# Moving the norms after the attention heads and the SSD into the load of the output projection, and adding the latents' expert rows in halves of 512 columns

## The chip, the core and the metric

The kernel runs on one core of a Trainium2 chip. The metric is the device time of one execution in microseconds; the median of three runs of the kernel before is 2430.44 us. TensorE (PE) does matrix products and transposes, VectorE (DVE), ScalarE (ACT) and GpSimd (POOL) do elementwise work, and SyncE (SP) issues most transfers. Each engine works through its own queue in order. 16 DMA engines move the data; transfers that add to memory or gather rows by an index are issued from POOL and have a queue of their own, the software queue.

## What is computed

Two layers over 512 latent tokens and 256 context tokens of width 1024. Each layer has a mixer and a mixture of experts. Cut to what matters here:

```python
o    = diff_attend(q, k_all, v_all, lam)                 # 4 heads, 128 wide: softmax 1 - lam * softmax 2
attn = rmsnorm(o, subln_w) * (1.0 - lam_init)            # a norm over each head's 128 columns
g    = (y * silu(z)).reshape(..., 2, 256)                # SSD output, gated, two groups
ssd  = g * rsqrt(mean(g * g) + EPS) * ssd_norm_w         # a norm over each group's 256 columns
x    = x + g1 * (concat([attn, ssd]) @ w_out)            # one output projection
x    = x + g2 * sum over experts of gate * down(silu(gate_proj(xe)) * up_proj(xe))
```

Each of 16 experts takes the 64 latent tokens and, in layer 0, the 32 context tokens that score highest, and its rows are added back at these tokens' places. Layer 1 needs no context output.

## The kernel before

**Order of the work.** Tokens lie in tiles of 128: tiles 0 to 3 are latents, 4 and 5 context. A mixer runs in stages: norm and transposes of the input, the columns of the SSD part, the gate `z`, then for each of four heads the projection (`Head.proj`), rotation (`Head.rope`) and attention (`Head.attend`), and at last the output projection (`op_tile`) with residual, norm and router. The order is made by hand: side work is written as generators, and `Slots.tick` advances every live generator by one step per tick while it puts the main products of the stage between them. A generator that yields `STEP` goes on within the same tick, so several chains of small operations are issued in turns. `attend` of head h runs during the projection of head h + 1, that of head 3 during the output projection.

**The root chain.** `rsqrt_steps` (L191 to L217) computes an inverse square root on VectorE in ten small dependent operations, with a `STEP` after each.

**The norms.** At the end of `attend`, ScalarE scales the head's 128 columns by the softmax's denominator (L1832) and sums their squares (L1834); a root chain `ors` on one column follows, and one VectorE operation multiplies by root and weight (L1837). The result is stored to `mixd` in DRAM; head 3's latent tiles are transposed and split at once instead. `z_out` (L1124) does the same for two groups of 256 SSD columns of one tile, with the chain `yrs` and two multiplies (L1135), which run beside the next chunk's `G` (L1072, L1074), the operand of `yd` on TensorE (L1081).

**The output projection.** `op_in` (L1180) loads a tile's mix from `mixd`, transposes it (`mtr`, L1192) and splits it in two float32r parts, hi and lo (L1194, L1196), since each product is three float32r products. It is queued for the next tile while this one is multiplied; the first tile's goes out as the stage starts. `w_out` comes through `Pieces`: ScalarE copies a piece of 128 x 512 to hi (L129), and POOL or VectorE, in turns, subtracts to get lo (L137). Products go over k in the order `OUT_ORDER`, SSD rows of `w_out` (k = 4 to 7) first, head rows (0 to 3) after.

**The experts.** `moe` streams all weights of each expert through SP's queue, in buffers that come free as TensorE uses them. The down projection `yl` (L1536) puts its 64 latent rows as two groups of 32 tokens by four column quarters of 256: each quarter has 32 partitions, the two groups lie side by side in 512 columns. `add_rows` (L1662) then scales one group's 128 x 256 by the gate and `G2` (L1665) and adds it with one indirect transfer of 128 rows of 1 KB (L1666). So an expert makes two such adds for the latents, one for the context in layer 0. Two adds to the same tensor wait for each other.

Of the kernel before, what the change touches and what calls it, by code (L numbers as in the profile page):

```python
# [8 lines left out]
F32 = mybir.dt.float32  # L9
F32R = mybir.dt.float32r  # L10
# [27 lines left out]
R_N1, R_N2, R_CW, R_CB, R_L = 0, 8, 16, 40, 48  # L38
# [26 lines left out]
OUT_ORDER = (4, 5, 6, 7, 0, 1, 2, 3)  # L65
# [47 lines left out]
class Pieces:  # L113
# [7 lines left out]
    def fetch(self):  # L121
        f = next(self.todo, None)
        if f:
            self.raw.append(f(self.net.rawp.tile([P, 512], F32, tag="raw", name="raw", bufs=4)))

    def pull(self, hi, lo):
        self.turn += 1
        nc, x = self.net.nc, self.raw.pop(0)
        nc.scalar.copy(hi.bitcast(F32R), x)  # L129
        self.flush()  # L130
        self.low = (nc.gpsimd if self.turn % 2 or x.shape[-1] == 384 else nc.vector), lo, x, hi

    def flush(self):

        if self.low:
            e, lo, x, hi = self.low
            e.tensor_tensor(lo.bitcast(F32R), x, hi, op=OP.subtract)  # L137
            self.low = None
            self.fetch()


class Net:
# [122 lines left out]
    def consts(self, p1):  # L265
# [8 lines left out]
        for l in range(2):  # L274
# [5 lines left out]
            self.lds(stack[b + R_CB:b + R_CB + 8], rows(I["conv_b"][l]))  # L280
        self.lds(self.rev, I["k_rev"])
# [89 lines left out]
    def pieces(self, l):  # L371
# [22 lines left out]

        cbs = [cb for g in range(2) for _, cb in GROUP[g]]
# [7 lines left out]
        for b in range(2):  # L403
            yield from (cols(w_out, k, 512 * b) for k in OUT_ORDER)

# [285 lines left out]
    def layer_params(self, l, lp, p1, lam_init):  # L691
# [7 lines left out]
        self.wsub = lp.tile([P, P], F32, name="wsub")  # L699
        self.wssd = lp.tile([P, 512], F32, name="wssd")  # L700
# [9 lines left out]
        ld(self.wsub, bc(I["subln_w"][l:l + 1], P))  # L710
        ld(self.wssd, bc(I["ssd_norm_w"][l:l + 1], 512))
# [6 lines left out]

        nc.vector.tensor_scalar(self.wsub, self.wsub, 1.0 - lam_init, None, op0=OP.mult)
# [404 lines left out]
    def z_out(self, l, t, ap):  # L1124

        nc, y = self.nc, self.Y[:, t]
        ss = ap.tile([P, 2], F32, tag="yss", name="yss", bufs=2)
# [8 lines left out]
        self.st(self.mixd[l][t * P:(t + 1) * P, 512:1024], y)  # L1136
# [43 lines left out]
    def op_in(self, l, t, op, psp):  # L1180
# [6 lines left out]
        self.mT[t] = mT = [op.tile([P, KD, P], F32, tag=f"mT{j}", name="mT", bufs=2) for j in range(2)]  # L1187
        yield
        for a, n in ((4, 4), (0, n)):
# [4 lines left out]
            nc.scalar.copy(mT[0][:, c].bitcast(F32R), tr)  # L1194
            yield STEP
            nc.vector.tensor_tensor(mT[1][:, c].bitcast(F32R), tr, mT[0][:, c], op=OP.subtract)  # L1196
# [124 lines left out]
    def route_open(self, l):  # L1321

        cst = self.cst
        self.gidx = cst.tile([96, NE], I32, name=f"gidx{l}") if l == 0 else None
        self.gidc = cst.tile([32, NE], I32, name=f"gidc{l}") if l == 0 else None
        self.sidx = cst.tile([P, 3, NE], I32, name=f"sidx{l}")
        self.gate = cst.tile([P, 3, NE], F32, name=f"gate{l}")
# [28 lines left out]
    def route_b(self, l, psp):  # L1356
# [25 lines left out]
        ps = psp.tile([P, 2, 2, NE], F32, tag="tr", name="sgp", bufs=3)  # L1382
        for g in range(2):
            for j in range(4):
                nc.tensor.matmul(ps[32 * j:32 * j + 32, g].rearrange("p i e -> p (i e)"), self.ident[0:64, 32 * g:32 * g + 32],
                                 c.rearrange("p i e -> p (i e)"), start=True, stop=True, skip_group_check=True)
        nc.vector.tensor_scalar(self.gate[:, 0:2], ps[:, :, 0], 0.5, None, op0=OP.mult)
        for j in range(4):
# [499 lines left out]
```

## Time and profile before

| | |
|---|---|
| median of 3 runs (lowest, highest) | 2430.44 us (2430.13, 2430.88) |
| the profiled execution's time | 2429.65 us |
| its span, first to last instruction | 2427.9 us |
| TensorE matmul busy | 2175.3 us, 90% |
| VectorE busy | 995.3 us, 41% |
| ScalarE busy | 635.9 us, 26% |
| POOL busy | 480.9 us, 20% |
| granted TensorE clock, mean | 0.964 |
| moved by DMA | 702.46 MB, 289 GB/s over the span |

Busy shares are means over stages that have different limits. A transfer's issue and its landing are two moments; what waits for a transfer waits for the landing. A wait that is put down to an engine is put down to what came last by the profile.

### The profile page before, as it was taken

What the parts mean: (1) busy time and instruction counts of PE and PEld (TensorE: products, weight loads), DVE (VectorE), ACT (ScalarE), POOL (GpSimd) and SP (SyncE); (2) the same over time, 40 slices, a digit from 0 to 9 for tenths busy, and PEclk for the clock granted to TensorE, in tenths of its full rate; (3) what the DMA queues carried; (4) which work ended last, traced back from release to release, by engine and by line L of the source; (5) the groups of instructions that cost most, each with busy time, mean ns of one, the idle gap of its engine ahead of it and who ended that gap; (6) DMA issues with size and microseconds to landing.
All of it is one profiled execution on the core that took longest, in us unless ns stands there. A gap on an engine that the chain in (4) does not pass through costs nothing. (4 is left out here: it accounts for less than half of the span.)

```text
span 2427.9 us, 55950 instructions
## 1 busy us (share of the span) xinstructions
PE 2175.3 (90%) x23460; PEld 1335.8 (55%) x23460; DVE 995.3 (41%) x3088; ACT 635.9 (26%) x1739; POOL 480.9 (20%) x584
## 2 busy tenths in 40 slices
PE   6898988998999999999987988989799999988775
PEld 4677787785445455455444667887543333333332
DVE  5789589873111111111116787887611111111010
ACT  4334467521111111111113443565111010101000
POOL 4464233100111101101103464241000001000001
PEclk9999999999999999999998998999899999999998
DMA  7322723678999999999994325324999999999997
GB/s 255 85 76 83 267 63 99 207 249 330 393 403 405 390 401 393 398 395 399 394 388 122 92 58 192 111 71 150 361 370 414 408 411 408 414 409 409 409 412 275
DMA packets 234759, 702.46 MB, mean 289 GB/s; under 512 B 30860, under 2 KB 88412, under 8 KB 234508
## 3 DMA queue, kind: packets, MB, share of 16 engines
q1 hardware_dynamic: 220428, 681.43, 72.6%
q0 software_dynamic: 14080, 17.46, 3.9%
q8 instruction: 185, 3.03, 0.5%
q14 instruction: 66, 0.54, 0.1%
HBM read 675.05 MB, written 23.76 MB: 288 GB/s over the span
## 5 line engine op out<-in xcount | busy, mean ns | idle before, releaser
L1490 PE MATMUL gl<-gw,xeT 128*32 128x512 f32 (+1 forms) x8192 | 655.6, 466 | 62.9 <-DMA gw<-w_up 62.7
L1490 PEld LDWEIGHTS gl<-gw,xeT 128*32 128x32 f32 x8192 | 277.7, 111 | 441.9 <-issue 404.3
L1529 DVE SCALAR_TENSOR_TENSOR th<-th,gl 128x256 f32<-128x256 f32 (+1 forms) x96 | 37.5, 391 | 702.9 <-ACT th L1528 702.9
L1536 PE MATMUL yl<-rt,hl 128*32 128x256 f32 x4080 | 247.5, 380 | 13.6 <-PE gl L1490 9.2
L1528 ACT ACTIVATE th<-gl 128x256 f32<-128x256 f32 (+1 forms) x96 | 35.1, 367 | 774.3 <-PE gl L1490 767.7
L171 PE MATMUL pacc<-rt,H 128*128 128x384 f32 (+1 forms) x768 | 206.3, 351 | 4.5 <-ACT V L1719 2.2
L1536 PEld LDWEIGHTS yl<-rt,hl 128*32 128x32 f32 x4080 | 134.1, 110 | 117.8 <-issue 16.0
L1666 POOL DMA_INDIRECT out<-ys,sidx x32 | 49.5, 1546 | 710.7 <-DVE ys L1665 599.1
L1665 DVE SCALAR_TENSOR_TENSOR ys<-yl,gate,G2l 128x256 f32<-128x256 f32 x64 | 28.0, 479 | 361.3 <-PE yl L1536 361.3
L1573 PE MATMUL gc<-gw,xeT 128*32 128x352 f32 x2048 | 170.6, 459 | 0.0
L171 PEld LDWEIGHTS pacc<-rt,H 128*128 128x128 f32 x768 | 137.8, 197 | 18.0 <-issue 6.3
L171 PE MATMUL xacc<-H,rt 128*128 128x512 f32 (+1 forms) x448 | 134.5, 376 | 6.8 <-ACT H L799 6.2
L171 PE MATMUL pacc<-rt,L 128*128 128x384 f32 (+1 forms) x384 | 130.0, 338 | 0.0
L1428 POOL DMA_INDIRECT xe<-xn2d,gidx x16 | 15.1, 944 | 529.4 <-PE xet L1438 389.8
L1443 ACT ACTIVATE xeT<-xet,MC,A 128x64 f32<-128x64 f32 (+1 forms) x256 | 74.3, 424 | 169.2 <-PE xet L1438 169.2
L137 POOL TENSOR_TENSOR rt<-raw,rt 128x384 fp32r<-128x384 f32 (+1 forms) x88 | 100.0, 1162 | 90.9 <-ACT rt L129 90.7
L171 PE MATMUL oacc<-woh,mT 128*128 128x512 f32 x304 | 107.2, 410 | 0.0
L1536 PE MATMUL yl<-wd,hl 128*32 128x256 f32 x1552 | 101.4, 382 | 4.4 <-DMA wd<-w_down 3.8
L1573 PEld LDWEIGHTS gc<-gw,xeT 128*32 128x32 f32 x2048 | 68.6, 110 | 56.2 <-issue 43.9
L171 PEld LDWEIGHTS xacc<-H,rt 128*128 128x128 f32 x448 | 82.2, 197 | 22.3 <-ACT H L799 7.0
L1666 POOL DMA_INDIRECT xr<-ys,sidx x32 | 49.9, 1560 | 194.9 <-DVE ys L1665 109.1
L1805 ACT ACTIVATE e<-sc,nm,rq 128x768 f32<-128x768 f32 (+1 forms) x80 | 72.1, 904 | 49.5 <-DVE nm L1801 46.9
(408 smaller groups left out, 3446.7 us busy)
## 6 DMA issues: line engine op xcount, KB each, us to landing
gw<-w_gate SPq DMA_DIRECT2D x256, 704.0 KB
gw<-w_up SPq DMA_DIRECT2D x256, 704.0 KB
rt<-w_down SPq DMA_DIRECT2D x255, 512.0 KB
wd<-w_down SPq DMA_DIRECT2D x97, 512.0 KB
mr<-w_mod SPq DMA_DIRECT2D x80, 512.0 KB
raw<-w_in SPq DMA_DIRECT2D x48, 256.0 KB
raw<-w_in SPq DMA_DIRECT2D x64, 192.0 KB
RB<-acsd SPq DMA_DIRECT2D x20, 512.0 KB
```

The costliest lines, as they stand in the source:

```text
L137: e.tensor_tensor(lo.bitcast(F32R), x, hi, op=OP.subtract)
L171: self.nc.tensor.matmul(o, a[x].bitcast(F32R), b[y].bitcast(F32R), start=start and i == 0, stop=stop and i == 2, **kw)
L1428: self.nc.gpsimd.indirect_dma_start(out=xe[0:n], out_offset=None, in_=self.xn2d[0:rows], in_offset=bass.IndirectOffsetOnAxis(ap=idx[0:n, e ...
L1443: nc.scalar.activation(xT[:, kk, c:d], tr[:, k, c - a:d - a], AF.Identity, scale=self.A2[:, s, kk:kk + 1], bias=self.MC[:, l, s, 24 + kk:2 ...
L1490: self.nc.tensor.matmul(gl[c][32 * j:32 * j + 32, o:o + n].rearrange("p (u t i) -> p u t i", u=2, i=32), self.xT[:, k, 32 * g:32 * g + 32] ...
L1528: nc.scalar.activation(th, g, AF.Tanh, scale=0.5)
L1529: nc.vector.scalar_tensor_tensor(th, th, 1.0, g, op0=OP.add, op1=OP.mult)
L1536: nc.tensor.matmul(y[32 * j:32 * j + 32], h[:, b], wd[b][:, 256 * j:256 * j + 256], start=new and b == 0, stop=b == NF - 1, skip_group_che ...
L1573: nc.tensor.matmul(gc[u][32 * j:32 * j + 32].rearrange("p (t i) -> p t i", i=32), xT[:, k, 64:96], w, start=k == 0, stop=k == KD - 1, skip ...
L1665: nc.vector.scalar_tensor_tensor(ys, y, self.gate[:, i, e:e + 1], G2, op0=OP.mult, op1=OP.mult)
L1666: nc.gpsimd.indirect_dma_start(out=dst, out_offset=bass.IndirectOffsetOnAxis(ap=self.sidx[:, i, e:e + 1], axis=0), in_=ys, in_offset=None, ...
L1805: nc.scalar.activation(ei[:, 0:w], sc[:, i * w:i * w + w], AF.Exp, scale=rq[:, t, i:i + 1], bias=nm[:, i:i + 1], accum_out=sm[:, i:i + 1])
```

## The change

`attend` and `z_out` no longer norm. They put the mean of the squares in a tile `mss` (128 x 6 tiles x 6 columns: two SSD groups, four heads) and store the bare values. `op_in` computes one root chain over all columns of its tile and scales the loaded mix, column group by column group, on ScalarE before it transposes. The weights go elsewhere: `ssd_norm_w` scales the SSD rows of `w_out` as they are staged, `subln_w` times 1 - lam_init scales the heads' columns after the transpose, where it lies along the partitions. Head 3's latent tiles keep a root chain of their own. `OUT_ORDER` takes SSD and head rows in turn. In the experts, the two halves of the down projection have 64 partitions each (32 per group) and 512 columns, and the latents' rows are added with one transfer of 128 rows of 2 KB. Two small VectorE operations of the attention are merged into their neighbours.

```diff
-OUT_ORDER = (4, 5, 6, 7, 0, 1, 2, 3)
+OUT_ORDER = (4, 0, 5, 1, 6, 2, 7, 3)
     def pull(self, hi, lo):
-        nc.scalar.copy(hi.bitcast(F32R), x)
+        if scale is None or scale is False:
+            nc.scalar.copy(hi.bitcast(F32R), x)
+        else:
+            nc.scalar.activation(hi.bitcast(F32R), x, AF.Copy, scale=scale)
...
+                e.scalar_tensor_tensor(lo.bitcast(F32R), x, scale, hi, op0=OP.mult, op1=OP.subtract)
...
     def consts(self, p1):
+            self.lds(stack[R_MIX + 5 * l:R_MIX + 5 * l + 1], rows(I["subln_w"][l]))
+            self.lds(stack[R_MIX + 5 * l + 1:R_MIX + 5 * l + 5], rows(I["ssd_norm_w"][l]))
...
     def layer_params(self, l, lp, p1, lam_init):
-        ld(self.wsub, bc(I["subln_w"][l:l + 1], P))
-        ld(self.wssd, bc(I["ssd_norm_w"][l:l + 1], 512))
...
     def z_out(self, l, t, ap):
-            nc.scalar.activation(junk, y[:, 256 * g:256 * g + 256], AF.Square, accum_out=ss[:, g:g + 1])
-        yield
-        rs = yield from self.rsqrt_steps(ap, ss, 2, 1.0 / 256, "yrs")
-        for g in range(2):
-            c = slice(256 * g, 256 * g + 256)
-            nc.vector.scalar_tensor_tensor(y[:, c], y[:, c], rs[:, g:g + 1], self.wssd[:, c], op0=OP.mult, op1=OP.mult)
+            nc.scalar.activation(junk, y[:, 256 * g:256 * g + 256], AF.Square, scale=1.0 / 16, accum_out=self.mss[:, t, g:g + 1])
         self.st(self.mixd[l][t * P:(t + 1) * P, 512:1024], y)
+        yield
...
     def op_in(self, l, t, op, psp):
-        yield
+        rs = yield from self.rsqrt_steps(op, self.mss[:, t, 0:n + 2], n + 2, 1.0, f"mrs{n}")
+        yield
+        cuts = [(512, 768), (768, D)] + [(P * h, P * h + P) for h in range(n)]
+        for i, (a, b) in enumerate(cuts):
+            nc.scalar.mul(mx[:, a:b], mx[:, a:b], rs[:, i:i + 1])
+            if i % 2:
+                yield STEP
...
+            else:
+                yield from self.head_split(mT[0][:, c], mT[1][:, c], tr)
+    def head_split(self, hi, lo, x):
+        w = self.wmix[:, 0:1]
+        self.nc.scalar.activation(hi.bitcast(F32R), x, AF.Copy, scale=w)
+        yield STEP
+        self.nc.vector.scalar_tensor_tensor(lo.bitcast(F32R), x, w, hi, op0=OP.mult, op1=OP.subtract)
...
     def route_b(self, l, psp):
-        ps = psp.tile([P, 2, 2, NE], F32, tag="tr", name="sgp", bufs=3)
-        for g in range(2):
-            for j in range(4):
+        ps = psp.tile([P, 2, NE], F32, tag="tr", name="sgp", bufs=3)
+        for j in range(2):
...
     def moe(self, l):
-        dst = [b.rearrange("n (j c) -> (n j) c", c=256) for b in base]
+        dst = [b.rearrange("n (j c) -> (n j) c", c=512 >> i) for i, b in enumerate(base)]
+        def down_lat(y, h, wd, b):
+            for j in range(2):
+                for g in range(2):
+                    nc.tensor.matmul(y[64 * j + 32 * g:64 * j + 32 * g + 32], h[:, g, b], wd[b][:, 512 * j:512 * j + 512],
+                                     start=b == 0, stop=b == NF - 1, skip_group_check=True)
...
-                    for g in range(2):
-                        down(y[:, 256 * g:256 * g + 256], hl[:, g], wd, b, g == 0)
+                    down_lat(y, hl, wd, b)
...
-                for g in range(2):
-                    self.add_rows(mw, y[:, 256 * g:256 * g + 256], g, e, G2[0], dst[0])
+                self.add_rows(mw, y, 0, e, G2, dst)
...
     def rope(self, a):
-        nc.vector.tensor_scalar(self.nrq[:, a:a + 2], rs[:, :, 0:2], -0.125, None, op0=OP.mult)
     def attend(self, t):
-        nc.vector.tensor_tensor(nm, nm, nrq[:, t], op=OP.mult)
+        nc.vector.scalar_tensor_tensor(nm, nm, -1.0, rq[:, t], op0=OP.mult, op1=OP.mult)
-        nc.vector.tensor_tensor(r2, sm[:, 0:1], rr[:, 1:2], op=OP.mult)
-        nc.vector.tensor_tensor(r2, r2, n.nlam, op=OP.mult)
+        nc.vector.scalar_tensor_tensor(r2, sm[:, 0:1], n.nlam, rr[:, 1:2], op0=OP.mult, op1=OP.mult)
...
-        nc.scalar.activation(junk, ob, AF.Square, accum_out=oss)
-        yield
-        ors = yield from n.rsqrt_steps(ap, oss, 1, 1.0 / P, "ors")
-        nc.vector.scalar_tensor_tensor(ob, ob, ors, n.wsub, op0=OP.mult, op1=OP.mult)
-        if self.h == 3 and not ctx:
+        nc.scalar.activation(junk, ob, AF.Square, scale=P ** -0.5, accum_out=oss)
+        yield
+        if own:
+            ors = yield from n.rsqrt_steps(ap, oss, 1, 1.0, "ors")
+            nc.vector.tensor_scalar(ob, ob, ors, None, op0=OP.mult)
```

## Rows read from the trace of the kernel before

**Rows 1.** The page: the span in 40 slices, tenths of DMA busy time.

```profile
DMA  7322723678999999999994325324999999999997
```

**Rows 2.** Busy time by stage; columns in the first row.

```profile
core 0: us, PE busy (x) PEld busy (x) DVE busy (x) ACT busy (x) POOL busy (x), PEclk, DMA share, GB/s
300.00:420.00 120.00, 105.57 (x709) 97.76 (x707) 105.78 (x390) 79.78 (x227) 43.50 (x66) 0.96 0.23 72
...
620.00:1240.00 620.00, 607.30 (x9069) 312.50 (x9065) 89.25 (x221) 84.50 (x273) 74.64 (x53) 0.99 1.03 398
...
1485.00:1640.00 155.00, 138.67 (x1005) 123.53 (x1003) 119.18 (x408) 86.21 (x239) 58.62 (x93) 0.95 0.41 134
...
1800.00:2400.00 600.00, 528.26 (x6571) 224.45 (x6563) 74.24 (x228) 58.19 (x171) 44.77 (x29) 0.99 1.03 410
```

**Rows 3.** TensorE's waits in four mixer stretches: us in total, times, longest.

```profile
PE yd L1081 <- DVE yrs_y L215: 2.6, 2, 2.1
...
PE wtr L1824 <- DVE QL L1778: 6.4, 3, 3.2
...
PE wtr L1824 <- DVE QL L1778: 5.8, 2, 3.4
...
PE mtr L1192 <- DMA mixin<-mixd: 3.2, 1, 3.2
```

**Rows 4.** Timeline, end: start, duration, engine, line, operation, [idle before <- releaser].

```profile
2412.99 0.87 DVE L1665 SCALAR_TENSOR_TENSOR ys<-yl,gate,G2l 128x256 f32<-128x256 f32 x2 [11.14 <-PE yl L1536]
2413.75 1.54 POOL L1666 DMA_INDIRECT out<-ys,sidx  x1 [33.37 <-DVE ys L1665]
2418.38 1.54 POOL L1666 DMA_INDIRECT out<-ys,sidx  x1 [3.09 <-DMA out<-ys,sidx]
```

**Rows 5.** Timeline, border between the layers.

```profile
1279.53 1.57 POOL L1666 DMA_INDIRECT xr<-ys,sidx  x1 [27.19 <-DVE ys L1665]
1284.15 1.56 POOL L1666 DMA_INDIRECT xr<-ys,sidx  x1 [3.05 <-issue]
1288.17 1.75 SPq L154 DMA_DIRECT2D xin<-xr  x4
1292.86 1.22 DVE L836 SCALAR_TENSOR_TENSOR junk<-xin 128x1024 bf16<-128x1024 f32 x1 [2.96 <-DMA xin<-xr]
```

**Rows 6.** DMA: 2034:2038 weights alone; 2043.59:2051.99 one add; 697.59:703.09 one gather.

```profile
DMA packets 341, 1.70 MB, mean 424 GB/s; under 512 B 40, under 2 KB 40, under 8 KB 341
...
q0 software_dynamic: 144, 0.13, 9.7%
...
q0 software_dynamic: 78, 0.32, 16.7%
```

**Rows 7.** Instructions by tile, xcount: ns min/median/max, first and last start.

```profile
L205 DVE TENSOR_TENSOR ors_e<-ors_e,ors_m x40: 150/159/1206, 286.7 to 1695.8; 128x1 f32<-128x1 f32 x40
...
L1837 DVE SCALAR_TENSOR_TENSOR ob<-ob,ors_y,wsub x40: 339/352/1435, 287.9 to 1698.1; 128x128 f32<-128x128 f32 x40
...
L1832 ACT ACTIVATE ob<-po,rr x40: 355/368/381, 283.3 to 1694.2; 128x128 f32<-128x128 f32 x40
```

**Rows 8.** Timeline, SSD gate of layer 1.

```profile
1452.02 0.97 DVE L196 TENSOR_SCALAR yrs_m<-yss 128x2 f32<-128x2 f32 x1
...
1461.16 0.15 DVE L215 SCALAR_TENSOR_TENSOR yrs_y<-yrs_e,yrs_y 128x2 f32<-128x2 f32 x1
...
1461.38 1.94 PE L1081 MATMUL yd<-XS,G 128*128 128x64 f32 x8 [7.29 <-DVE yrs_y L215]
```

**Rows 9.** Timeline, output projection of layer 1, last tile's mix.

```profile
1698.73 0.80 SPq L154 DMA_DIRECT2D mixin<-mixd  x2
...
1710.87 0.63 PE L1192 MATMUL mtr<-ident,mixin 128*128 128x128 f32 x4
```

**Rows 10.** Chain that ended last, start of that projection: start, us, what.

```profile
1636.46 4.54 DMA mixin<-mixd
...
1641.13 1.73 PE mtr L1192 x7
```

More of the change, by code (lines that the diff above doesn't have):

```diff
@@ L403, in pieces @@
         for b in range(2):
-            yield from (cols(w_out, k, 512 * b) for k in OUT_ORDER)
+            yield from (scaled(cols(w_out, k, 512 * b), k - 4) if k > 3 else plain(cols(w_out, k, 512 * b)) for k in OUT_ORDER)
     def staged(self, W, ws, n, hi=None):
@@ L1325, in route_open @@
         self.gidc = cst.tile([32, NE], I32, name=f"gidc{l}") if l == 0 else None
-        self.sidx = cst.tile([P, 3, NE], I32, name=f"sidx{l}")
-        self.gate = cst.tile([P, 3, NE], F32, name=f"gate{l}")
+        self.sidx = cst.tile([P, 2, NE], I32, name=f"sidx{l}")
+        self.gate = cst.tile([P, 2, NE], F32, name=f"gate{l}")
     def affinities(self, l, t, n):
@@ L1507, in moe_open @@
         self.wp = self.tc.alloc_tile_pool(name=f"wd{l}", bufs=1, reuse_waits="tile", side="right")
-        self.G2 = [mw.tile([P, 256], F32, name="G2" + "lc"[s]) for s in range(2 if ctx else 1)]
+        self.G2 = [mw.tile([P, 512 >> s], F32, name="G2" + "lc"[s]) for s in range(2 if ctx else 1)]
         for s in range(2 if ctx else 1):
@@ L1530, in act, with down @@
             nc.vector.tensor_tensor(h, th, u, op=OP.mult)
-        def down(y, h, wd, b, new=True):
+        def down(y, h, wd, b):
             for j in range(4):
                 nc.tensor.matmul(y[32 * j:32 * j + 32], h[:, b], wd[b][:, 256 * j:256 * j + 256],
-                                 start=new and b == 0, stop=b == NF - 1, skip_group_check=True)
+                                 start=b == 0, stop=b == NF - 1, skip_group_check=True)
+        def down_lat(y, h, wd, b):
+            for j in range(2):
+                for g in range(2):
+                    nc.tensor.matmul(y[64 * j + 32 * g:64 * j + 32 * g + 32], h[:, g, b], wd[b][:, 512 * j:512 * j + 512],
+                                     start=b == 0, stop=b == NF - 1, skip_group_check=True)
         xe = None
@@ L1656, in add_last @@
         nc, (ys, g2) = self.nc, self.ytail
-        nc.scalar.activation(ys, y, AF.Copy, scale=self.gate[:, 2, e:e + 1])
+        nc.scalar.activation(ys, y, AF.Copy, scale=self.gate[:, 1, e:e + 1])
         nc.gpsimd.tensor_tensor(ys, ys, g2, op=OP.mult)
-        nc.gpsimd.indirect_dma_start(out=dst[1], out_offset=bass.IndirectOffsetOnAxis(ap=self.sidx[:, 2, e:e + 1], axis=0),
+        nc.gpsimd.indirect_dma_start(out=dst[1], out_offset=bass.IndirectOffsetOnAxis(ap=self.sidx[:, 1, e:e + 1], axis=0),
                                      in_=ys, in_offset=None, compute_op=OP.add)
@@ L1663, in add_rows @@
         nc = self.nc
[L1664 to L1666 removed]
+        ys = mw.tile([P, 512 >> i], F32, tag=f"ys{i}", name="ys", bufs=2)
+        nc.vector.scalar_tensor_tensor(ys, y, self.gate[:, i, e:e + 1], G2[i], op0=OP.mult, op1=OP.mult)
+        nc.gpsimd.indirect_dma_start(out=dst[i], out_offset=bass.IndirectOffsetOnAxis(ap=self.sidx[:, i, e:e + 1], axis=0),
                                      in_=ys, in_offset=None, compute_op=OP.add)
@@ L1693, in open @@
         self.rq = ap.tile([P, NT, 2], F32, tag="rq", name="rq", bufs=2)
-        self.nrq = ap.tile([P, NT, 2], F32, tag="nrq", name="nrq", bufs=2)
         nq = T if self.full else S
@@ L1841, in attend @@
             nc.tensor.transpose(tr, ob, n.ident)
-            n.split(*([m[:, t] for m in n.oT] if n.oT else [m[:, 3] for m in n.mT[t]]), tr)
+            yield from n.head_split(*([m[:, t] for m in n.oT] if n.oT else [m[:, 3] for m in n.mT[t]]), tr)
             return
```

69 lines of the change are left out of this document (39 added, 30 removed).

## The prediction

> **What bounds the kernel now.** I read the 40 slices first. Their DMA line stands at 9 through two long stretches, the two expert stages, and falls to 2 to 7 through most of the two mixers [rows 1]: two kinds of stage with two different limits. The table by stage, read next, says which resource binds where [rows 2]. In the expert stages the DMA share is 1.03, so no engine of the 16 ever rests, at 398 GB/s in layer 0 and 410 GB/s in layer 1. Such a stage ends when its bytes are through: a later start or a byte more moves its end, an idle engine does not. In layer 0 TensorE is nearly full too, 607.3 of 620 us, so a lighter stream can give at most the 12.7 us that it idles there. In the head stages TensorE works 105.6 of 120 us and 138.7 of 155 us with VectorE at 105.8 and 119.2: TensorE leads, and what it loses it loses mostly to VectorE's queue. The waits by pair name it: the transposes `wtr` wait 6.4 and 5.8 us for `QL`, a VectorE result [rows 3]. Each expert stage starts when the mixer before it lets it, so time saved in a mixer goes through to the end.
>
> **The sum, part by part.** It is made against the profiled execution: 2429.65 us, span 2427.9, 0.79 below the median of 2430.44.
>
> *1. The last add of the program.* The last expert's two halves are scaled in 0.87 us together; the first add is issued at 2413.75, and the second only when the first has landed, at 2418.38 [rows 4]. One add of 512 columns waits for both halves of the scaling (2412.99 + 0.87, and the 0.27 that lay between scaling and issue), so it goes out at 2414.13. That is 2418.38 - 2414.13 = 4.2 us earlier. The same row count is written with twice the bytes each; the landing may be some tenths longer. -4.2 (bounds -4.6 and -3.4).
>
> *2. The border between the layers.* The same pair stands at 1279.53 and 1284.15, and the loads of `xin` on SP's queue follow at 1288.17, after the second add has landed; VectorE's first square waits 2.96 us for such a load until 1292.86 [rows 5]. With one add, issued 0.4 us later than the first was, the loads go out about 1284.1 + 0.4, 3.7 us earlier. VectorE still has the last context expert's activation ahead of it, which ends just before that wait began, so no more than those 2.96 us come through. -3.0 (bounds -3.7 and 0).
>
> *3. The streams.* An add takes queue time from the weights. In the 8.4 us around one add the software queue holds 9.7% of 16 engines, 13.0 us for 128 rows of 1 KB: 102 ns a row. A gather of 4 KB rows holds 16.7% of 5.5 us, 14.7 us for 78 packets: 188 ns. Weights alone run at 424 GB/s, 26.5 a DMA engine, 39 ns per KB [rows 6]. Two adds per expert cost 2 x 128 x 102 ns / 16 = 1.63 us of the stream. What a row of 2 KB costs as an add isn't in the trace. If all of the 102 ns belong to the row, one add costs half and 0.82 us per expert are saved; if all belong to the bytes, nothing. Between them: one more KB at 39 ns makes 141 ns and saves 0.50; read and written back, two times 39 more, it makes 180 ns and saves 0.19. I take 0.35, between these two. 30 experts lie in the streams (the last of each layer is in parts 1 and 2): -10.5 (bounds -24.5 and 0). The down projection issues half as many matmuls of twice the width into the same four column groups; I cost it at nothing, since the stream covers it. If it ran 10% off either way it would show only in layer 0's 12.7 us.
>
> The Trainium skill, "DMA: Bandwidth & Descriptors", section Specifications, speaks against this part: it puts the smallest transfer for line rate at 512 B, so rows of 1 KB would already run as fast as the engine can and wider ones gain nothing. The trace does not agree at 1 KB, for this accumulating write at least: 102 ns against the 39 that 1 KB takes among the weights. By the rule the term is 0, by the row it is -10.5.
>
> *4. SSD gate.* `z_out` loses, in 10 tiles (6 + 4), ten root steps of about 0.16 us [rows 7] and two multiplies over 256 columns. They stand in VectorE's queue between the pieces of the next chunk's `G`, which `yd` on TensorE waits for: 7.29 us at 1461.38, put down to the root chain, whose first step starts at 1452.02 and whose last ends at 1461.31 [rows 8]. VectorE never rests between; from each step's start to that of the next instruction the ten take 3.9 us. In layer 0 waits of `yd` are put down to the chain with 2.6 us [rows 3]. The two squares stay, on ScalarE; the store of `Y` comes earlier. -6 (bounds -9 and 0).
>
> *5. Heads.* 32 of 40 `attend` calls lose a chain of ten steps of 159 ns and a multiply of 352 ns [rows 7]: at most 1.94 us each, less where two chains interleave. 18 of them lie in layer 0's head stage and 12 in layer 1's, 35 and 23 us at most, against 105.8 and 119.2 us that VectorE works there [rows 2]. One further small operation goes in each of the 40 calls (`r2`) and 24 times in `rope` (`nrq`). Off the path all this is worth nothing; on it, it can give at most TensorE's idle time, 14.4 and 16.3 us. I take somewhat over half of the waits for `QL` [rows 3], whose work stands behind such chains: -4 and -3, together -7 (bounds -16 and 0).
>
> *6. The load of the output projection.* Added: 10 chains of n + 2 columns (10 x 10 steps of some 0.16 us against 42 x 10 removed) and 52 ScalarE scalings, five or six per tile. A 128-wide ScalarE scaling by a column takes 368 ns [rows 7]; two of 256 lie between that and twice that, so a latent tile pays 1.8 to 2.6 us; I take 2.1. For later tiles this is covered: the mix is requested at 1698.73 and transposed at 1710.87 [rows 9], 12.1 us for a load that takes 4.5 [rows 10]. The first tile has no cover: its transposes start at 1641.13, as the load lands [rows 10], and TensorE has idled 3.2 us for it [rows 3]. Two things change there. The store of head 2's rows, for which this load waits, no longer follows a root chain and its multiply; that is ten steps of 159 ns and 352 ns [rows 7] with gaps, so store and load come some 2 to 3 us earlier. But the new chain stands among the steps of `rope` on VectorE, and behind the scalings on ScalarE wait the copies of `w_out` pieces and the last head's exponentials, which TensorE needs. Gain 2 to 3, price 2.1 plus a chain of 2 to 5 that partly runs while the load does: between -1 and +4 per layer. I take +1.5, so +3.
>
> *7. At nothing.* Staging `w_out`: half of its pieces get a scale on ScalarE, and VectorE's subtraction becomes a multiply and subtract at the same width; neither engine leads in the output projection. The order of k alternates the halves, but both are transposed before the first product either way. Four small loads more on POOL's queue at the start, while it waits for weights; two broadcasts fewer on POOL, two fewer on SP at the border. Three scalings of routing indices and twelve small matmuls fewer, after the choice of experts. A tenth of a microsecond each, either sign.
>
> Sum: -4.2 - 3.0 - 10.5 - 6 - 7 + 3 = -27.7, so 2402 us by the profiled execution's time and 2402.7, rounded 2403, by the median.
>
> **Rivals.**
> A. *The stream gains nothing* (an add's cost goes with its bytes). For it: an add row of 1 KB costs more than twice what 1 KB of weights does, as if it moved its bytes more than once. Against it: the gather's 188 ns for 4 KB. Time: 2403 + 10.5 = 2413. The Trainium skill's rule in part 3 leads to the same time.
> B. *An add costs by its rows*: layer 0 gets at most the 12.7 us, layer 1 15 x 0.82 = 12.3, so -24.5 in place of -10.5: 2389.
> C. *VectorE's work was not what TensorE waited for*: the small steps filled gaps, and the queues are ordered so that other results come no earlier. For it: the waits for `QL` are less than half of what TensorE idles in the head stages [rows 2, 3]. Parts 4 and 5 fall away: 2403 + 13 = 2416.
> D. *Slower: the scalings stand on the path of every tile.* Mechanism: mix, chain, scalings, transposes and split in a row on three queues for each of the 10 tiles, ahead of that tile's products. Price: 2.1 + ten steps with their gaps, 1.9, is 4.0 per tile, 40 us in place of the 3 of part 6: 2403 + 37 = 2440. It decides from 3.1 us per tile on, where it eats all the rest. Against it: the 12.1 us between request and transpose; for it: ScalarE runs its queue in order, and a scaling that waits for its load holds the copies behind it.
>
> **How the numbers follow.** Forecast 0.50, A 0.15, B 0.12, C 0.12, D 0.11. The measurement can tell about 0.2%, 4.9 us, from no change. A, B and C are all faster by more than that; A and C together would give 2426, at the edge, and I put 0.06 on such mixtures as no change, taken from A and C. Slower is D, 0.11 with 0.01 off for its mild form: faster 0.84, same 0.06, slower 0.10. The range reaches from below B, with the heads at their bound, to A and C together: 2384 to 2426; D lies outside.
>
> **What would show it.** Each step has its place in the profile after: one add per expert for the latents, and at the end one between scaling and the last landing; the `xin` loads about 4 us after the last add of layer 0; the software queue's share around one add (part 3: about 23 us of engine time for 128 rows if a row takes 180 ns, 18 if 141, 13 if rival B holds); no wait of `yd` for a root chain; shorter waits of `wtr` for `QL`; the first `mtr` no later against the last projection of head 3 than 3 us more, and no wait of later `mtr` for a scaling. The prediction is wrong if the expert stage takes as long as before (A), if the mixers do (C), or if TensorE waits before each tile's transposes (D).

## The result, and the profile after

The changed kernel takes 2391.27 us (median of 4 runs, 2388.69 to 2393.27) against 2430.28 us of the kernel before on the same chip (2428.93 to 2430.88). The ratio is 0.984, 95% interval 0.9824 to 0.9855: 35 to 43 us faster, 39 in the middle. 2403 were forecast, 27.7 us faster. The profiled execution has a span of 2388.0 us and a time of 2389.74.

**Where the 40 us of the span went.** I took the same landmarks in both traces (first and last start of an operation) and cut the span into stretches between them. The differences add up to 40.0 us, the 39.9 between the spans but for rounding:

| stretch | before, us | after, us | difference | forecast |
|---|---|---|---|---|
| start to first `xacc` | 29.6 | 31.4 | +1.8 | 0 |
| `xacc`, both layers | 226.1 | 227.1 | +1.0 | 0 |
| last `xacc` to last `pacc` (gate, SSD, heads), layer 0 | 258.9 | 242.3 | -16.6 | -13 in |
| the same, layer 1 | 220.4 | 204.5 | -15.9 | both |
| last `pacc` to first `oacc`, both layers | 25.5 | 30.0 | +4.5 | +3 |
| first `oacc` to first add, both layers | 339.7 | 339.2 | -0.5 | 0 |
| first add to last expert's first add (streams) | 1281.9 | 1274.9 | -7.0 | -10.5 |
| border: that add of layer 0 to first `xacc` of layer 1 | 31.7 | 29.1 | -2.6 | -3.0 |
| that add of layer 1 to the end | 14.1 | 9.4 | -4.7 | -4.2 |

The end, the border and the load of the output projection came out nearly as forecast. The streams gave less. The gate, SSD and head stretches gave two and a half times what was forecast.

Each row is one execution. The kernel of experiment 10 below is the changed kernel up to the first add of layer 1, and its trace has 452.1 us in the two gate, SSD and head rows where the kernel after has 446.8, and 344.6 us from first `oacc` to first add in place of 339.2. So some 5 us in such a row are what two executions can differ by, and the +1.8 and +1.0 tell nothing. The streams, the border and the end repeat better: 1274.1 to 1277.9, 27.9 to 29.2 and 9.2 to 9.4 us in the traces of the experiments that leave them alone.

The page after, first the engines, then granted clock and DMA in 40 slices:

```profile
PE 2176.3 (91%) x20620; PEld 1247.0 (52%) x20620; DVE 931.7 (39%) x2586; ACT 652.2 (27%) x1791; POOL 433.5 (18%) x554
...
PEclk9999999999999999999998999999899999999999
DMA  7323723589999999999994226334999999999997
```

The shape is that of [rows 1]: two expert stages with every slice at 9, two mixers between. VectorE works 63.6 us less over the span.

The ends of the stretches in the timeline after (start, duration, engine, line, operation, idle before and its releaser): border, start and end of layer 1's experts, end of the program.

```profile
1260.76 1.55 POOL L1700 DMA_INDIRECT xr<-ys,sidx  x1 [36.56 <-DVE ys L1699]
...
1265.76 2.58 SPq L162 DMA_DIRECT2D xin<-xr  x4
...
1765.52 1.61 POOL L1700 DMA_INDIRECT out<-ys,sidx  x1 [140.74 <-DMA rt<-w_down]
...
2377.56 0.75 DVE L1699 SCALAR_TENSOR_TENSOR ys<-yl,gate,G2l 128x512 f32<-128x512 f32 x1 [10.22 <-PE yl L1572]
2378.59 1.54 POOL L1700 DMA_INDIRECT out<-ys,sidx  x1 [40.97 <-DVE ys L1699]
```

Against [rows 4] there is one add behind one scaling, and the span ends 9.4 us after it, as it ended 9.5 us after the second one before. Against [rows 5] the loads of `xin` follow 5.0 us after the first add, not 8.6.

One add in the stream, the 8.4 us from 1975.60 (software queue: packets, MB, share of 16 engines), and the expert stages by windows:

```profile
q0 software_dynamic: 144, 0.26, 16.9%
```

```profile
606.00:1220.00 614.00, 603.32 (x7856) 268.39 (x7852) 87.86 (x209) 86.08 (x279) 52.90 (x39) 1.00 1.03 401
...
1766.00:2360.00 594.00, 535.02 (x5300) 188.34 (x5296) 71.10 (x210) 56.94 (x168) 22.76 (x15) 0.99 1.02 410
```

16.9% of 16 engines in 8.4 us are 22.7 us of engine time, 177 ns for each of 128 rows of 2 KB, where a row of 1 KB took 102 [rows 6]. An expert's latent adds so cost 1.42 us of the stream in place of 1.63.

TensorE's waits after in the mixers (us in total, times, longest): SSD gate of layer 0, its heads and output projection, then the same two of layer 1:

```profile
PE yd L1098 <- DVE G L1091: 4.7, 4, 3.5
...
PE sc L1828 <- DVE rope L1784: 4.7, 1, 4.7
...
PE mtr L1210 <- ACT mixin L1204: 2.2, 1, 2.2
PE wtr L1855 <- DVE QL L1810: 0.2, 1, 0.2
...
PE yd L1098 <- DVE G L1091: 5.9, 2, 5.2
...
PE mtr L1210 <- ACT mixin L1204: 8.0, 1, 8.0
...
PE wtr L1855 <- DVE QL L1810: 0.2, 1, 0.2
```

The waits of `wtr` for `QL`, 6.4 and 5.8 us before, are 0.2 us each. No `yd` waits for a root chain; what is left are its waits for `G`. In layer 0 it had such waits before, too:

```profile
PE yd L1081 <- DVE G L1074: 7.1, 3, 6.3
```

With this row the waits of `yd` for `G` and the chains were 7.1 and 2.6 us in layer 0 and 7.3 in layer 1 [rows 8], 17.0 in all, and are 10.6 after. The first `mtr` of a layer waits for a scaling, 2.2 and 8.0 us, and in layer 0 the scores of the output projection wait 4.7 us for a step of the rotation (`rope`).

**The head stretches, split.** Busy time from the last `xacc` to the last `pacc`, layer 0 and layer 1 (columns as in [rows 2]: us; PE, PEld, DVE, ACT, POOL busy; PEclk; DMA share; GB/s), the kernel before:

```profile
154.20:413.10 258.90, 236.12 (x1480) 196.93 (x1479) 208.40 (x737) 137.28 (x393) 97.26 (x143) 0.95 0.35 116
1412.60:1633.00 220.40, 194.53 (x1272) 168.76 (x1271) 175.48 (x567) 110.20 (x307) 93.65 (x135) 0.95 0.34 108
```

and the kernel after:

```profile
154.90:397.20 242.30, 228.29 (x1480) 195.17 (x1479) 172.28 (x455) 135.96 (x393) 97.19 (x143) 0.98 0.38 124
1393.40:1597.90 204.50, 188.59 (x1272) 163.63 (x1271) 152.77 (x385) 109.16 (x306) 92.41 (x134) 0.97 0.37 117
```

The first count shows that TensorE does the same 1480 and 1272 matmuls. Its idle time (length less busy) falls from 48.7 to 29.9 us, 18.8 less; but its busy time falls too, from 430.6 to 416.9, 13.8 less, at a granted clock of 0.98 and 0.97 in place of 0.95. VectorE's busy time falls from 383.9 to 325.1.

### The profile page after: what moved, and what is told of

It reads as the page before. It is cut to its first block, busy times and chain, and to the rows that moved or that the text cites. A ratio compares the mean times of both kernels' runs of the same rounds, so it can differ in the third digit from the quotient of the medians.

```text
span 2388.0 us, 49731 instructions
## 1 busy us (share of the span) xinstructions
PE 2176.3 (91%) x20620; PEld 1247.0 (52%) x20620; DVE 931.7 (39%) x2586; ACT 652.2 (27%) x1791; POOL 433.5 (18%) x554
## 5 line engine op out<-in xcount | busy, mean ns | idle before, releaser
L1572 PE MATMUL yl<-rt,hl 128*32 128x512 f32 x2040 | 257.7, 595 | 9.5 <-PE gl L1518 9.2
L1558 ACT ACTIVATE th<-gl 128x256 f32<-128x256 f32 (+1 forms) x96 | 35.1, 366 | 768.1 <-PE gl L1518 761.4
L1699 DVE SCALAR_TENSOR_TENSOR ys<-yl,gate,G2l 128x512 f32<-128x512 f32 x32 | 24.0, 751 | 380.5 <-PE yl L1572 367.4
L1700 POOL DMA_INDIRECT out<-ys,sidx x16 | 24.8, 1549 | 730.6 <-DVE ys L1699 589.8
L1572 PEld LDWEIGHTS yl<-rt,hl 128*32 128x32 f32 x2040 | 70.4, 109 | 141.3 <-issue 83.2
L1572 PE MATMUL yl<-wd,hl 128*32 128x512 f32 x776 | 102.2, 599 | 2.2 <-DMA wd<-w_down 1.7
L179 PE MATMUL xacc<-L,rt 128*128 128x512 f32 (+1 forms) x224 | 82.6, 371 | 3.0 <-POOL L L879 2.1
L1485 PE MATMUL xpk<-x,one 128*64 128x512 f32 x256 | 81.8, 633 | 3.4 <-DVE one L1481 3.4
```

Source lines behind the costliest of these rows:

```text
L179: self.nc.tensor.matmul(o, a[x].bitcast(F32R), b[y].bitcast(F32R), start=start and i == 0, stop=stop and i == 2, **kw)
L1485: nc.tensor.matmul(ps[64 * j:64 * j + 64], one[:, t], self.x1[t][:, 512 * j:512 * j + 512], start=t == 0, stop=t == NL - 1, skip_group_che ...
L1558: nc.scalar.activation(th, g, AF.Tanh, scale=0.5)
L1572: nc.tensor.matmul(y[64 * j + 32 * g:64 * j + 32 * g + 32], h[:, g, b], wd[b][:, 512 * j:512 * j + 512], start=b == 0, stop=b == NF - 1, s ...
L1699: nc.vector.scalar_tensor_tensor(ys, y, self.gate[:, i, e:e + 1], G2[i], op0=OP.mult, op1=OP.mult)
L1700: nc.gpsimd.indirect_dma_start(out=dst[i], out_offset=bass.IndirectOffsetOnAxis(ap=self.sidx[:, i, e:e + 1], axis=0), in_=ys, in_offset=No ...
```

## Experiments

My theory after the comparison: TensorE waited for VectorE's queue in the heads, where the root chains stood in front of what it needs, and paid for each long wait a second time at half its clock; the adds give some 12 us. The rivals: the SSD gate alone, the later store of the rows, the merged small operations or the new order of instructions carry the gain, or the adds do. Each kernel was compared with the kernel before on the same chip; there and in the section on the result that one took 2429.6 to 2430.3 us, so the changed kernels' times are set side by side as they are.

**1. The adds alone.** The kernel before with the hunks of `route_open`, `route_b`, `G2_load`, `moe`, `add_last` and `add_rows`, of which this is the heart:

```diff
-                for g in range(2):
-                    self.add_rows(mw, y[:, 256 * g:256 * g + 256], g, e, G2[0], dst[0])
+                self.add_rows(mw, y, 0, e, G2, dst)
```

> The kernel before with the latents' adds by halves and nothing else. My theory, from the landmarks of the two traces: the adds give 4.5 us at the end, 2.5 at the border of the layers and 2.5 in each stream, 12 in all, so a ratio of 0.995 to before (2418 us). The rival that adds cost by their rows (102 ns each) gives 24.5 + 7 = 31 us (2399); the rival that they cost by their bytes gives only the end and the border, 7 us (2423). In layer 0 the last latent add should be issued about 4 us earlier than before, counted from the first add of that layer.

2413.84 us, ratio 0.9935 (0.9921 to 0.9949): 16 us faster, 12 to 19. Neither of the two rivals fits, and my 12 lies at the edge. In its trace the streams are 4.1 and 3.3 us shorter, the border 3.8, the end 4.8: 16.0 in all, a little over the 14.3 of the same rows in the table above. (The traced execution took 2419.99 us, 6 more than the median; it lost 5.2 from first `oacc` to first add, a row that varies by as much.) The gate, SSD and head stretches are as before, 479.5 us in sum against 479.3. So the rest of the change's 39 us, some 23, is the deferral's, with the merged operations.

**2. The heads' chains put back**, with their multiply and the store behind them:

```diff
+        ors = yield from n.rsqrt_steps(ap, oss, 1, 1.0, "ors")
+        nc.vector.scalar_tensor_tensor(ob, ob, ors, ob, op0=OP.mult, op1=OP.max)
         n.st(n.mixd[self.l][t * P:(t + 1) * P, P * self.h:P * self.h + P], ob)
```

> The changed kernel with the root chain and one multiply of 128 columns put back behind the squares in the 32 attend calls that lost them, the store behind them (those rows are scaled twice). If these chains in VectorE's queue are what held TensorE in the head stages, this gives back most of the 28 us that the two SSD and head stretches lost: 18 to 22 us (2409 to 2413), TensorE idle up by some 6 us per layer between last gate product and last projection, and TensorE busy up by some 4 us per layer for the same 1261 and 1120 matmuls, at a lower granted clock. If the gain came from the SSD gate, the merged small operations or the new order of instructions, it gives back under 6 us.

2409.21 us, ratio 0.991 (0.9894 to 0.9925): 18 us of the 39 are given back. The two stretches take 464.3 us, 17.5 more than after the change: 12.2 of it idle and 5.3 busy time of TensorE, for 33.9 us more of VectorE's. TensorE's waits in layer 1 name VectorE's queue again:

```profile
PE po L1860 <- DVE rr L1845: 4.6, 1, 4.6
PE wtr L1855 <- DVE QL L1810: 3.4, 1, 3.4
```

The place can be seen in the kernel before. VectorE's timeline in the heads of layer 0, the end of one chain and the next one:

```profile
341.21 0.16 DVE L215 SCALAR_TENSOR_TENSOR ors_y<-ors_e,ors_y 128x1 f32<-128x1 f32 x1
341.41 0.35 DVE L1837 SCALAR_TENSOR_TENSOR ob<-ob,ors_y,wsub 128x128 f32<-128x128 f32 x1
341.68 1.75 DVE L1800 TENSOR_REDUCE nm<-sc 128x2 f32<-128x1536 f32 x1
...
345.06 0.15 DVE L196 TENSOR_SCALAR ors_m<-oss 128x1 f32<-128x1 f32 x1 [1.11 <-ACT oj L1834]
...
348.47 0.34 DVE L1837 SCALAR_TENSOR_TENSOR ob<-ob,ors_y,wsub 128x128 f32<-128x128 f32 x1
348.84 0.86 DVE L1776 TENSOR_TENSOR KK<-qtr,KK 64x256 fp32r<-64x256 f32 x2
349.71 0.88 DVE L1778 TENSOR_TENSOR QL<-qtr,Q 64x256 fp32r<-64x256 f32 x2
```

Behind the first `ob` stands the maximum of the scores, without which the softmax doesn't begin; behind the second stand `KK` and `QL`, without which the next scores don't. The chain itself makes VectorE idle: at 345.06 it waited 1.11 us for the squares on ScalarE, with everything behind it.

One count has to be set right. VectorE's instructions over the span rise from 2586 to 2970, twelve for each of the 32 calls. So a root chain is eleven instructions and not ten (the step at L198 and L199 has two). VectorE's busy time rises by 43.4 us over the span, 33.9 of it in the stretches. The expectations to 7, 9 and 11 divide by 32 x 1.94 = 62 us in its place, a sum of durations of instructions that overlap, and their rates of 0.26 and 0.29 us per us are too low for that reason.

**3. The SSD gate's chains put back**, with the two multiplies:

```diff
+        rs = yield from self.rsqrt_steps(ap, self.mss[:, t, 0:2], 2, 1.0, "yrs")
+        for g in range(2):
+            c = slice(256 * g, 256 * g + 256)
+            nc.vector.scalar_tensor_tensor(y[:, c], y[:, c], rs[:, g:g + 1], y[:, c], op0=OP.mult, op1=OP.max)
```

> The changed kernel with the root chain over two columns and the two multiplies of 256 columns put back in the SSD gate, the store behind them (those rows are scaled twice). My theory: 6 to 9 us are given back (2397 to 2400), with a wait of yd for a chain again. If the SSD gate, not the heads, carries the gain of the two stretches, 15 us or more. If other VectorE work is late there in any case, under 2.

2398.71 us, ratio 0.9871 (0.9856 to 0.9886): 7.4 us given back, as my theory had it. The stretches take 455.8 us, 9.0 more, of which 5.9 is busy time of TensorE, for 19.0 us more of VectorE's. In layer 1 `yd` waits for the chain again:

```profile
PE yd L1098 <- DVE yrs_y L223: 6.7, 1, 6.7
```

**4. An earlier root for the projection's first tile.** The chain runs during the projection of head 3:

```diff
+                    if h == 3 and tk == 11:
+                        q.add(self.early_root(l))
...
+        self.root0 = yield from self.rsqrt_steps(self.lp, self.mss[:, 0, 0:5], 5, 1.0, "mr0")
...
```

> The changed kernel with the root chain of the projection's first tile computed earlier, during the projection of head 3, so that only load and scalings stand before its transposes. TensorE idles 8.0 us (layer 1) and 4.7 + 2.2 us (layer 0) there, and the chain ends 4 to 5 us after the load has landed. If the chain is what is late: 3 to 5 us in layer 1 and 1 to 3 in layer 0, 4 to 8 us faster than the change (2383 to 2387), first mtr then behind the load. If ScalarE's queue or the load is as late: within 1 us of the change.

2391.09 us, ratio 0.9842 (0.9829 to 0.9856): no different from the change. The first `oacc` does follow the last `pacc` sooner, after 13.4 and 13.9 us in place of 15.4 and 14.6, but layer 0's projection then takes 128.8 us in place of 124.3. Next late is ScalarE's queue. Its timeline in this kernel, layer 1:

```profile
1604.05 0.99 ACT L1846 ACTIVATE e<-sc,nm,rq 128x768 f32<-128x768 f32 x1 [1.75 <-DVE nm L1842]
...
1605.04 0.98 ACT L1846 ACTIVATE e<-sc,nm,rq 128x768 f32<-128x768 f32 x1
...
1606.26 1.79 ACT L1213 ACTIVATE mixin<-mixin,mr_y 128x256 f32<-128x256 f32 x5
```

The scaling's root was ready at 1603.6, 2.6 us before; it stands behind two exponentials, which waited for the maximum of the scores on VectorE. My guess that the chain alone was late fell.

**5. Both sets of chains put back.** The edits of 2 and 3 together.

> The changed kernel with both sets of chains and multiplies put back, in the SSD gate and behind the heads (their rows are scaled twice). What is left of the change against the adds alone is then the load of the output projection with its chain and scalings, the weights folded in and the merged small operations. If the two parts add up: 2391 + 18 + 7.5 = 2416 to 2417, which is 2 to 3 us above the adds alone (2414), the net price of the projection's load. If they share one slack, so that either alone already takes part of it: 2420 or more. If one covers the other: under 2412.

2414.13 us, ratio 0.9935 (0.9922 to 0.9947): the adds alone over again (2413.84). The parts nearly add up, 18 + 7.4 against 23; and what is left of the deferral (the load of the projection, the weights folded in, the new order of k and of instructions, the merged operations) comes to nothing in sum, within the few us that two such kernels' times can tell.

**6. The heads' chains put back loose**, behind the store, into a spare tile that nobody reads:

```diff
+        ors = yield from n.rsqrt_steps(ap, oss, 1, 1.0, "ors")
+        spare = ap.tile([P, P], F32, tag="spare", name="spare", bufs=1)
+        nc.vector.scalar_tensor_tensor(spare, ob, ors, ob, op0=OP.mult, op1=OP.max)
```

> The changed kernel with the heads' chains and multiplies put back, but into a spare tile, behind the store and with no reader. If the instructions in VectorE's queue are what TensorE waits for, this costs the same as with the store behind them: 15 to 20 us, 2406 to 2411. If it is the later store of the rows and what waits for it: within 2 us of the change (2389 to 2393).

2407.23 us, ratio 0.9907 (0.9894 to 0.992): 16 us given back by work whose result nobody wants. So it is the work in VectorE's queue that costs, not the store.

**7. The merged operations taken apart:**

```diff
+        nc.vector.tensor_scalar(self.nrq[:, a:a + 2], rs[:, :, 0:2], -0.125, None, op0=OP.mult)
...
-        nc.vector.scalar_tensor_tensor(nm, nm, -1.0, rq[:, t], op0=OP.mult, op1=OP.mult)
+        nc.vector.tensor_tensor(nm, nm, nrq[:, t], op=OP.mult)
...
```

> The changed kernel with the merged small operations taken apart again (24 of rope's and 40 of attend's put back, about 0.16 us each). 64 x 0.16 is 10 us of VectorE time. At the rate of the heads' chains (18 us given back for 32 x 1.94 = 62 us put back, 0.29) it gives back 3 us: 2394. If they stand where TensorE waits for the very result (nm before the exponentials, r2 before the weights): 5 to 8 us. If nothing waits for them: under 1.

2393.05 us, ratio 0.9855 (0.9837 to 0.9872): 2 us, near the 3 expected, but the interval holds 0 too.

**8. Waits filled.** Transposes of the identity keep TensorE at work in four waits:

```diff
+        if g and c == 2:
+            self.warm((18, 28)[l])
         yd = self.scp.tile([P, 256], F32, tag="x", name="yd", bufs=3)
...
```

> The changed kernel with TensorE kept at work in four of its waits by transposes of the identity that nobody reads: 18 and 28 before the late yd of each layer (waits of 3.5 and 5.2 us), 26 at the first scores of the output projection of layer 0 and 44 before the first mtr of layer 1 (waits of 4.7 and 8.0 us). Nothing else gets shorter. If a wait also costs what TensorE then does at half its clock (the granted clock was 0.52 and 0.63 in the 8 us behind the wait of layer 1), each place gives 1 to 2 us: 4 to 7 us faster than the change, 2384 to 2387, with yd and yo at half their durations there. If the waits alone are the price: within 1 us of the change, or slower by what the transposes stick out.

2394.74 us (2386.79 to 2401.22), ratio 0.9854 (0.9834 to 0.9873): no gain that can be told, against my theory's 4 to 7 us. What it shows it shows in place. In the kernel after, layer 1, `yd` and `yo` behind the wait:

```profile
1438.11 1.94 PE L1098 MATMUL yd<-XS,G 128*128 128x64 f32 x8 [5.19 <-DVE G L1091]
1439.84 2.02 PE L1103 MATMUL yo<-H,Cc 128*128 128x512 f32 x2
```

and with the wait filled:

```profile
1435.64 3.22 PE L1147 MATMUL warm<-ident 128*128 128x128 f32 x28
1441.04 1.08 PE L1100 MATMUL yd<-XS,G 128*128 128x64 f32 x8 [2.18 <-DVE G L1091]
1441.95 1.08 PE L1105 MATMUL yo<-H,Cc 128*128 128x512 f32 x2
```

The same matmuls take about half as long. From the last `zacc` to the first `pacc` it is 1.2 and 1.3 us less, from the last `pacc` to the first `oacc` 0.6 and 1.4, 4.5 us in four places. As much was lost elsewhere: the gate products of layer 1 took 36.7 us in place of 35.1, its heads 159.1 in place of 157.1, layer 0's stream 663.4 in place of 661.8. The edit puts nothing into these, and the times of this kernel spread over 14 us. Whether filling pays stays open.

**9. The loose chains twice.** The edit of 6 with the chain and its multiply issued two times.

> The changed kernel with the chains and multiplies behind the heads put back twice, into a spare tile, with no reader. Once gave 16 us more than the change (2407 against 2391) for 32 x 1.94 = 62 us of VectorE work, 0.26 us per us. If TensorE pays for VectorE's queue in proportion, twice gives 32 us: 2421 to 2426. If a limit lies between (VectorE becomes the bound), more: 2430 and up. If the first one only used up a slack that the change had made and the second finds other gaps: under 2415.

2439.99 us, ratio 1.0028 (1.0006 to 1.005): 49 us given back, more than twice 16. By the trace the second set isn't dearer where the first one was: the gate, SSD and head stretches take 479.3 us, 12.6 more than with one set, for 26.2 us more of VectorE's. Another 17 us lie in layer 0's output projection, where the context tiles of head 3 are attended: 143.2 us against 126.0 with one set, with a wait of 8.1 us for VectorE before a transpose:

```profile
PE obt L1873 <- DVE ob L1870: 8.1, 1, 8.1
```

So in the stretches the cost stays in proportion, and the excess is another stage's, which the expectation left out.

**10. Every latent add of layer 1 once more**, to a tensor that nobody reads any longer:

```diff
+        if len(dst) == 1:
+            nc.gpsimd.indirect_dma_start(out=self.xr[0].rearrange("n (j c) -> (n j) c", c=512),
...
```

> The changed kernel with every latent add of layer 1 issued a second time to a tensor that nobody reads any more (128 rows of 2 KB again, 16 more). One add holds 22.7 us of engine time (177 ns a row), 1.42 us on each of 16 engines. If the stream pays for an add with its engine time, as the forecast took it: 15 x 1.4 = 21 us in the stream, and some 4 us at the end for the second landing: 2412 to 2418. If the stream has slack for adds: under 2400. If adds hold the weights up by more than their own time: 2425 and up.

2412.87 us, ratio 0.9919 (0.9893 to 0.9946): 21.6 us more than the change. The first and the last expert's adds:

```profile
1773.13 1.61 POOL L1700 DMA_INDIRECT out<-ys,sidx  x1 [140.71 <-DMA rt<-w_down]
...
2403.93 1.54 POOL L1700 DMA_INDIRECT out<-ys,sidx  x1 [40.70 <-DVE ys L1699]
2405.78 1.54 POOL L1703 DMA_INDIRECT xr<-ys,sidx  x1 [0.30 <-issue]
```

630.8 us lie between the first two of these, against 613.1 after the change: 17.7 us over 15 experts, 1.18 us an add. An add's engine time, 1.42 us, goes to the stream for five sixths; some 3 us more come at the end.

**11. More taken off VectorE.** The sum of the two softmax parts goes over ScalarE and POOL:

```diff
-        nc.vector.scalar_tensor_tensor(e[0][:, 0:w], e[1][:, 0:w], r2, e[0][:, 0:w], op0=OP.mult, op1=OP.add)
+        nc.scalar.mul(e[1][:, 0:w], e[1][:, 0:w], r2)
+        nc.gpsimd.tensor_tensor(e[0][:, 0:w], e[0][:, 0:w], e[1][:, 0:w], op=OP.add)
...
```

> The changed kernel with a further piece of VectorE's work in the heads taken off it: the sum of the two softmax parts (one operation of 1.02 us over 768 columns in each latent attend, 40 in all) becomes a scaling on ScalarE and an addition on POOL, with a second buffer for the second part. By the rate of the heads' chains (0.26 to 0.29 us per us of VectorE work) 41 us taken off give 10 to 12 us: 2379 to 2381. If the longer way over two engines, or ScalarE's queue with the copies that TensorE waits for, takes the lead: 2391 and up.

2405.65 us, ratio 0.9886 (0.9847 to 0.9925): 14 us slower than the change. (Of the 40 operations 32 have 768 columns; the 8 of the context tiles have 256.) VectorE works 17.6 us less in the stretches, though 27.5 us of these operations left it there, and the stretches are 16.0 us longer: POOL takes 1.83 us for an addition that was part of a 1.02 us operation, and TensorE now waits for POOL, 4.7 us in layer 1 in place of 0.7:

```profile
PE pacc L179 <- POOL rt L143: 4.7, 5, 2.0
```

Less work on VectorE gains only if it isn't put on another queue that TensorE waits for.

No experiment gave a version that beats the changed kernel.

## Why the prediction was right and where it was not

The direction and the forecast's mechanisms were right, and the time lies in the range, but one term was too small by more than half. The misses partly cancel: part 3 was taken 3.5 us too large, part 5 some 11 too small. By its time alone, 2391, the change would speak for rival B (2389) more than for the forecast (2403); it takes the stretches and experiments 1 and 2 to tell that B's 24.5 us from the streams did not come and that the gate, SSD and heads gave 32.5 where 13 were forecast. Point by point:

- **Parts 1 and 2** (end -4.2, border -3.0): the table shows -4.7 and -2.6. At the border I was right by the length, not by the place: VectorE's first square comes 15.2 us after the add, not earlier than the 13.3 before, and the gain shows only between it and the first `xacc`.
- **Part 3** (streams -10.5): too large; the table shows -7.0, 0.23 us an expert. What failed is the choice between the two models of an add's row. The prediction left "about 23 us of engine time for 128 rows if a row takes 180 ns, 18 if 141"; it is 22.7, the dearer one, which by itself would have given 0.19 an expert. So an added row costs nearly by its bytes. Rival B (-24.5) fails by the table's -7.0 and by experiment 1, in which the adds gave 16 in all, end and border with them; rival A (nothing) would have left the streams as long as before. The Trainium skill, "DMA: Bandwidth & Descriptors", section Specifications, with line rate from 512 B on, would have had 0 here; per KB the row went from 102 to 89 ns and not further down to the 39 of the weights, so the trace agrees neither with the rule nor with a cost by rows; the rule's 0 misses the -7.0 by more than the forecast did.
- **Part 4** (SSD gate -6): experiment 3 gives back 7.4, and the waits of `yd` fell by 6.4. Right.
- **Part 5** (heads -7): this is the term that was mis-sized. Experiment 2 gives back 18, 17.5 of it in the two stretches, past the part's own bound of 16. "Somewhat over half of the waits for `QL`" was a wrong reading: the waits put down to `QL` were only one name for VectorE's queue. `nm`, `rr` and `KK` stand in the same queue; with the chains put back, the longest wait in layer 1's heads, 4.6 us, is one of `po` for `rr`. And "at most TensorE's idle time, 14.4 and 16.3 us" is no true ceiling. The 17.5 us lie below its 30.7, but 5.3 of them are not idle time: TensorE's busy time isn't fixed, and over the whole change the same matmuls took 13.8 us less in the two stretches.
- That last point by the rows: in layer 1 before, TensorE waited from 1454.1 to 1461.4 [rows 8]. Windows before, in (two) and behind that wait:

```profile
1442.00:1454.00 12.00, 12.00 (x62) 9.51 (x60) 10.37 (x27) 5.75 (x17) 7.07 (x8) 1.00 0.06 16
1454.00:1458.00 4.00, 0.09 (x1) 0.00 (x0) 4.00 (x8) 2.26 (x6) 3.92 (x6) 1.00 0.37 100
1458.00:1462.00 4.00, 0.62 (x3) 0.65 (x4) 4.00 (x11) 1.31 (x5) 1.88 (x2) 0.54 0.53 142
1462.00:1466.00 4.00, 4.00 (x18) 2.97 (x18) 2.47 (x6) 1.70 (x6) 2.59 (x4) 0.61 0.50 151
```

  The granted clock is 1.00 before the wait and in the first row of the wait, and 0.54 in the second, near its lower level of 1.2 GHz; behind the wait TensorE is busy without a gap and at 0.61 in the mean. The Trainium skill, "TensorE: Matmul & The Clock Gate", Part 1, says that the throttled clock is the resting state and that activity lifts it; these rows and experiment 8 agree.
- **What a step costs** was taken as 159 ns, the median. In the trace before, that holds while POOL computes nothing: 449 of the 550 instructions of the root chains in the heads and the SSD gate overlap no elementwise operation of POOL's, and none of them takes over 0.17 us. Of the other 101 more than half take over 0.3, up to 1.21 [rows 7]. In the wait of [rows 8], two steps and the POOL work beside them:

```profile
1457.00 0.94 DVE L207 SCALAR_TENSOR_TENSOR yrs_q<-yrs_e 128x2 f32<-128x2 f32 x1
1458.95 0.94 DVE L209 SCALAR_TENSOR_TENSOR yrs_y<-yrs_q,yrs_y 128x2 f32<-128x2 f32 x1
```

```profile
1456.89 2.99 POOL L137 TENSOR_TENSOR rt<-raw,rt 128x384 fp32r<-128x384 f32 x3
```

  All chains together take 114.8 us, where 550 times 0.159 are 87.5. So a part of what the chains cost is time that they stood beside POOL's work; how much of the gain that is, no experiment separates.
- **Part 6** (load of the output projection +3): +4.5 in place, within its bounds. The first tile waits 2.2 and 8.0 us for its scaling. Experiment 4 shows that the chain wasn't the only late thing: 2.8 us gained between these landmarks did not show in the whole time.
- **Rival C** (VectorE's work was not what TensorE waited for) is refuted by experiments 2, 3 and 6. **Rival D** (a scaling on the path of every tile) did not come: of all `mtr` only the first of each layer waited for a scaling.

One rate would have done better than the list of waits. In the gate, SSD and head stretches, with VectorE's busy time and the length from one view:

| kernel | VectorE busy, us | stretches, us | us per us of VectorE, against the kernel after |
|---|---|---|---|
| after | 325.1 | 446.8 | |
| 3, SSD chains back | 344.1 | 455.8 | 0.47 |
| 2, heads' chains back | 359.0 | 464.3 | 0.52 |
| 6, the same, loose | 360.3 | 466.7 | 0.57 |
| 5, both back | 378.3 | 474.8 | 0.53 |
| before | 383.9 | 479.3 | 0.55 |
| 9, loose twice | 386.5 | 479.3 | 0.53 |

Over this whole range about half a us of the stretch goes with each us of VectorE. The row of 3 alone is weak, since its 9.0 us are not far above the 5 by which two executions can differ. Experiment 11 does not follow the rate, for there the work went to POOL. The forecast's 13 us for the 58.8 us that it removed there were a rate of 0.22.

## What to carry to other kernels

Where two engines are both busy for 80 to 90% of a stage, price work removed from the second one by the stage (so much of its length per us of that engine, here about half), not by the waits that carry the name of one result; an undo of one part measures the rate at once. Don't take an engine's idle time as the ceiling of a gain where its clock falls in waits: its busy time shrinks too. Moving work to a third queue is another matter than removing it, as experiment 11 shows. And a time that lies in the range, or that agrees with a rival, says little until the stretches are compared.

## What the runs showed of the hardware

- An accumulating indirect transfer took 102 ns of engine time for a row of 1 KB and 177 ns for one of 2 KB, where 1 KB among the weights takes 39. One more such add per expert lengthened a stream at 406 GB/s by 1.18 us, of 1.42 us of engine time.
- Behind a wait of some 5 us eight `yd` matmuls took 1.94 us and two `yo` 2.02; with the wait mostly filled by transposes of the identity both took 1.08.
- The root chains' instructions on VectorE, on one or two columns, took at most 0.17 us while POOL computed nothing (449 in the trace before), and up to 1.21 us beside an elementwise operation of POOL's (101).
